# Dealing PEER's gathered rows out among the gate groups, and streaming the modulation matrix through MLPs and GLA

## The chip, the core and the metric

The kernel runs on one core of a Trainium2 chip. The time is the device microseconds of one execution; the profiled execution also has a span in its trace, from the first to the last instruction. TensorE is PE (its weight loads PEld), VectorE DVE, ScalarE ACT, GpSimd POOL, and SyncE, which issues most DMAs, SP.

## The reference

The program is two small networks in a row, batch 1, 256 positions, width 1024, all in fp32. The first has two layers (attention and MLP, then gated linear attention and MLP); the second two layers of a gated mixer and PEER, an expert layer that picks 16 of 16384 experts for each of 8 heads. Layer `l` of the second is modulated by a vector made from `c`:

```python
ada = (c @ w_ada[l] + b_ada[l])[:, None, :]
sh1, sc1, g1, sh2, sc2, g2 = jnp.split(ada, 6, axis=-1)
h = rmsnorm_2(x, norm1_g[l]) * (1.0 + sc1) + sh1
...                                             # mixer: x = x + g1 * (merged @ w_out[l])
h = rmsnorm_2(x, norm2_g[l]) * (1.0 + sc2) + sh2
x = x + g2 * peer(h, w_query[l], sub_keys[l], expert_u[l], expert_v[l])
# peer, per token t, over its picked experts (index idx, gate g):
u = jnp.take(expert_u, idx, axis=0); vv = jnp.take(expert_v, idx, axis=0)
a = jax.nn.gelu(jnp.einsum("td,thkd->thk", h, u))
out = jnp.einsum("thk,thkd->td", g * a, vv)
```

## The kernel before

**Weights.** Every weight comes in chunks of 128x1024 fp32 (`chunk`, L157 to L167): SP loads `raw` (4 buffers), ACT casts it to `whi` (L164), DVE subtracts to get `wlo` (L165; 3 buffers each), and PE runs three matmuls in place of one, hi by hi, hi by lo, lo by hi (L170 to L172). PE can't start a chunk's lo part before DVE has written `wlo`, and ACT can't cast chunk n before PE has left chunk n - 3.

**PEER.** Its experts are 128 blocks of 128. Positions 0 to 223 are computed densely: for each block, `u_block` makes all 128 dot products (24 matmuls of 224 columns) and ACT applies gelu into `A`; then the gates, zero for the experts that weren't picked, are multiplied into `A` (L1223); then `v_block` splits two blocks of `A` into hi (ACT, L223) and lo (DVE, L224), in `yh` and `yl`, and adds the products up in PSUM. The gates of 8 positions at a time are built by a group: three DVE operations (L1204, L1207, L1211), 16 small matmuls (L1221, L1222) and the multiplication; 28 groups for each half of the experts, listed in pairs. The last 32 positions go another way: 32 times, one row of `expert_u` is gathered for each of 128 (position, pick) pairs by an indirect DMA that POOL issues (L1113, tile `rows`, 3 buffers), and DVE makes a dot product of it with `hN` (L1124); `row_gates` applies gelu and the gates; 32 gathers of `expert_v` follow, which DVE adds up in `hN` (L1133, L1135); `rows_out` brings the sums into PSUM. The order is: 64 U blocks (U1), beside which DVE picks experts (top-16 steps, L941 to L945, and what follows); 64 U blocks (U2) beside the gates of the first half; 64 V blocks (V1) beside the gates of the second; 60 V blocks (V2); a tail of four whose chunks are loaded into buffers of their own.

**What sets the order around the change.** Side work waits in a list of steps, each with a cost (`Bg`). Each weight chunk adds a share (`U1_SHARE`, `MLP_SHARE`, ...) to a credit, and steps are taken off the front while the credit covers them; `flush` takes all that is left at once. A dot or a sum costs 1.05 and asks for the gather of two dots later when it is taken; the first three gathers are asked for together, and a step of 2.0 that does nothing follows them. A scheduler then places every engine's instructions with this program order as its priority. What is in the lists: in U1, the pick steps; in U2, the first half's gates, then 18 dots; in V1, the second half's gates; in V2, the 14 other dots, `row_gates` and 32 sums.

**The modulation vector.** `ada_steps` makes it from 96 chunks of `w_ada`, 48 a layer, in the same `raw` buffers: SP loads a chunk, and DVE multiplies it by `c` and adds up (L737) in one instruction; a second one reads the sum. A step costs 1.14. Layer 0's 48 steps run in both MLPs beside the weights' chunks; layer 1's are split, 36 from the second half of the last MLP through mixer 0, 12 at the end of the first PEER's V2. GLA (`gla`) sets the list aside for one of its own, which `flush` empties before its attention part; there, DVE's state updates (L674) and masked products (L682, L685) feed PE (L696).

Of the kernel before, what the change touches and what calls it, by code (L numbers as in the profile page):

```python
# [20 lines left out]
T = 256  # L21
# [19 lines left out]
MIX_SHARE = 0.45  # L41
U1_SHARE = 1.2
U2_SHARE = 1.25
V1_SHARE = 1.0
V2_SHARE = 0.9
DOTS1 = 18
ADA1 = 36
GSCALE = 2.0 ** 15
# [51 lines left out]
class Net:  # L100
# [378 lines left out]
    def mlp(self, l):  # L479
        nc, a = self.nc, self.a  # L480
        with ExitStack() as st:
# [23 lines left out]
            if l == 0:  # L505
                self.next_norm(self.gain(1))
            else:
                self.bg.flush()
                self.ada_steps(1, 0, ADA1, self.cb)
                self.next_norm(self.gg, self.modc(0, 0), self.tot2, self.gain(4))  # L510
# [3 lines left out]
    def gla(self):  # L514
        nc, a, c, tc = self.nc, self.a, self.cst, self.tc
        with ExitStack() as st:
# [119 lines left out]
            def ev_r(half):  # L636
# [9 lines left out]
                return go  # L646

            for half in range(2):
                ci = self.lin_nat(a["wgin"], ci, 512, self.yh, self.yl, ev_v(half), 1.2)
# [75 lines left out]
            self.next_norm(self.gain(3))  # L725
            self.lin(a["wgo"], 0, 8, 8, oh, ol, self.add_x, n=T)


    def ada_steps(self, l, i0, i1, cb):
        nc, a = self.nc, self.a  # L730
        cols = slice(l * 48, l * 48 + 48)

        def one(i):
            def go():
                raw = self.sp.tile([P, 1024], F32, tag="raw", name="raw", bufs=4)
                nc.sync.dma_start(out=raw, in_=a["wada"][i])
                nc.vector.tensor_tensor_reduce(out=raw, in0=raw, in1=cb, op0=ALU.mult, op1=ALU.add, scale=1.0,  # L737
                                               scalar=0.0, accum_out=self.mod[:, i : i + 1])
            return go

        def fin():
            nc.vector.tensor_add(out=self.mod[:, cols], in0=self.mod[:, cols], in1=self.cst["bada"][:, cols])
            for k, gi in ((1, 5), (4, 7)):
                m = self.modc(l, k)
                nc.vector.scalar_tensor_tensor(out=m, in0=m, scalar=1.0, in1=self.gain(gi + l),
                                               op0=ALU.add, op1=ALU.mult)
            if l == 0:
                nc.vector.tensor_mul(out=self.gg, in0=self.gain(4), in1=self.modc(0, 1))
        self.bg.add([(1.14, one(i)) for i in range(l * 48 + i0, l * 48 + i1)] + [(0.3, fin)] * (i1 == 48))

# [273 lines left out]
    def peer(self, l):  # L1024
        nc, a, c, tc = self.nc, self.a, self.cst, self.tc
        V = nc.vector
        with ExitStack() as st:
# [63 lines left out]
            def h_rows():  # L1091
# [7 lines left out]
                for k0 in (0, 4):  # L1099
# [5 lines left out]
                    nc.scalar.copy(out=hN[:, k0 * P : k0 * P + 512], in_=m)  # L1105

            def rows_of(name, use):

# [36 lines left out]
            with ExitStack() as s0:  # L1145
# [33 lines left out]
                self.wys.close()  # L1179
            self.bg.add(self.pick_steps(tm, fin))  # L1180

# [74 lines left out]
            self.set_banks(range(2, 8))  # L1256
            self.bg.add(gate_steps(0))
            dots = rows_of("un", dot)
            self.bg.add(dots[: DOTS1 + 2])
            for i2 in range(HALF, NI2):  # L1260
                u_block(i2, U2_SHARE)
            self.bg.flush()
            self.bg.add(gate_steps(1))
            vacc = [self.bank(2 + i).rearrange("p (k t) -> p k t", k=2) for i in range(4)]
# [8 lines left out]
            V.tensor_scalar_mul(g2s, self.modc(l, 5), 1.0 / GSCALE)  # L1273
            self.bg.add(dots[DOTS1 + 2 :] + [(0.5, row_gates)] + rows_of("ev", add_rows) + [(0.0, rows_out)])
            if l == 0:
                self.ada_steps(1, ADA1, 48, self.load(vp, "cb", eng=nc.sync))
            for i2 in range(HALF, NI2 - VTAIL):
# [36 lines left out]
    def run(self):  # L1314
# [10 lines left out]
        for name, f in stages:  # L1325
            f()
            if name == "att":
# [4 lines left out]
                cb = self.load(pool, "cb")  # L1332
                self.ada_steps(0, 0, 48, cb)
                self.cb = cb
            if name == self.stop:
# [139 lines left out]
```

## Time and profile before

| | us |
|---|---|
| median of three runs | 2587.16 |
| lowest and highest of them | 2585.8 and 2591.28 |
| the profiled execution | 2591.03 |
| its span in the trace | 2589.2 |
| PE busy in the span | 2526.5 |
| DVE busy in the span | 2112.0 |

PE is busy nearly all the time, so a view that averages over the span says little; the views to read are those of short stretches, where PE is idle or its granted clock is below 1.00. Matmuls overlap, so their single durations don't add up to time; how many of them run in a stretch does. In the trace the stages stand at: attention 0 to 95, MLP 95 to 295, GLA to 440, MLP to 640, mixer 0 to 800, PEER 0 to 1600 (U1 860 to 1034, U2 to 1222, V1 to 1415, V2 to 1585), mixer 1 to 1780, PEER 1 to the end.

### The profile page before, as it was taken

To read this page: it belongs to the slowest core of one execution; us is meant where nothing else is said; L and a number is where in the kernel's file an instruction comes from. 1 tells how busy PE (TensorE), PEld (TensorE's weight loads), DVE (VectorE), ACT (ScalarE), POOL (GpSimd) and SP (SyncE) were. 2 spreads that over 40 slices of the span, in tenths; PEclk is the share of its full clock that TensorE was granted. 3 is DMA by queue.
4 is the path that set the end of the run, shared out by engine and by line. 5 is a ranking of instruction groups with operands and counts; after the bars stand their busy time and mean duration, and the time that the engine had idled before them with its cause. 6 is when DMAs were issued, how large, how long until landed. Compare 5 with 4: busy or idle time off the path is not lost.

```text
span 2589.2 us, 55162 instructions
## 1 busy us (share of the span) xinstructions
PE 2526.5 (98%) x22496; PEld 2471.4 (95%) x22496; DVE 2112.0 (82%) x3835; ACT 1307.3 (50%) x2035; POOL 205.5 (8%) x172
## 2 busy tenths in 40 slices
PE   8999999999999999999999998999999999999998
PEld 7899988999999999999999997999999999999998
DVE  7787687877887798788887888778798788888886
ACT  6654475545546545444444544646545444444444
POOL 0000100000000000003000341000000002100341
PEclk9999999999999999999999998999999999999999
DMA  5288753876576566657656898465566667766895
GB/s 189 98 290 276 239 163 123 286 270 230 179 263 204 175 195 205 197 176 276 220 180 197 319 344 292 147 187 191 170 197 195 204 180 257 237 184 180 302 349 194
DMA packets 155918, 567.00 MB, mean 219 GB/s; under 512 B 17696, under 2 KB 17920, under 8 KB 155408
## 3 DMA queue, kind: packets, MB, share of 16 engines
q1 hardware_dynamic: 135792, 491.49, 58.7%
q0 software_dynamic: 19872, 71.99, 7.8%
q8 instruction: 176, 2.88, 0.5%
q14 instruction: 78, 0.64, 0.1%
HBM read 562.36 MB, written 1.05 MB: 218 GB/s over the span
## 4 chain that ended last, share of the span: by engine, by line
PE 74%; issue 15%; DMA 6%; DVE 3%; ACT 1%; POOL 1%; SPq 0%; DVEq 0%; POOLq 0%; ACTq 0%
PE b L170 23%; PE b L171 23%; PE b L172 23%; DMA rows<-in_ev,idx 3%; DVE wlo L165 1%; POOL rows L1113 1%; DMA raw<-in_wada 1%; DMA A<-in_sel 1%; ACT whi L164 1%; PE b L1169 1%; DMA rows<-in_un,idx 1%; DVE hN L1135 1%; PE b L1221 1%; PE b L1222 0%; PE b L825 0%
## 5 line engine op out<-in xcount | busy, mean ns | idle before, releaser
L170 PE MATMUL b<-yh,whi 128*128 128x224 f32 (+3 forms) x5336 | 1486.1, 279 | 12.6 <-ACT whi L164 9.0
L171 PE MATMUL b<-yl,whi 128*128 128x224 f32 (+3 forms) x5336 | 1480.1, 278 | 12.0 <-DVE yl L224 11.9
L172 PE MATMUL b<-yh,wlo 128*128 128x224 f32 (+3 forms) x5336 | 1481.1, 278 | 2.2 <-DVE wlo L165 2.2
L164 ACT CAST whi<-raw 128x1024 fp32r<-128x1024 f32 x829 | 867.9, 1049 | 1145.9 <-PE b L171 978.6
L165 DVE TENSOR_TENSOR wlo<-raw,whi 128x1024 fp32r<-128x1024 f32 x829 | 1010.8, 1221 | 245.3 <-ACT whi L164 237.9
L170 PEld LDWEIGHTS b<-yh,whi 128*128 128x128 f32 (+1 forms) x5336 | 1024.3, 192 | 16.8 <-ACT whi L164 9.5
L171 PEld LDWEIGHTS b<-yl,whi 128*128 128x128 f32 (+1 forms) x5336 | 1025.7, 192 | 15.3 <-DVE yl L224 12.6
L172 PEld LDWEIGHTS b<-yh,wlo 128*128 128x128 f32 (+1 forms) x5336 | 1024.3, 192 | 4.9 <-DVE wlo L165 3.4
L1113 POOL DMA_INDIRECT rows<-in_un,idx x64 | 82.9, 1295 | 1207.3 <-DVE wS L1124 759.5
L171 PE MATMUL b<-hl,whi 128*128 128x256 f32 x512 | 144.9, 283 | 0.0
L170 PE MATMUL b<-hh,whi 128*128 128x256 f32 x512 | 144.9, 283 | 0.0
L172 PE MATMUL b<-hh,wlo 128*128 128x256 f32 x512 | 144.9, 283 | 0.0
L737 DVE CUSTOM_DVE_ANT_0 raw<-raw,c_cb 128x1024 f32<-128x1024 f32 x96 | 117.1, 1220 | 7.5 <-DMA raw<-in_wada 7.3
L1113 POOL DMA_INDIRECT rows<-in_ev,idx x64 | 98.5, 1538 | 123.4 <-DVE hN L1135 92.4
L1223 DVE TENSOR_TENSOR A<-A,b 128x512 f32<-128x512 f32 x112 | 74.2, 684 | 36.9 <-PE b L1222 36.7
L171 PEld LDWEIGHTS b<-hl,whi 128*128 128x128 f32 x512 | 98.3, 192 | 0.0
L172 PEld LDWEIGHTS b<-hh,wlo 128*128 128x128 f32 x512 | 98.3, 192 | 0.0
L170 PEld LDWEIGHTS b<-hh,whi 128*128 128x128 f32 x512 | 98.3, 192 | 0.0
L1135 DVE SCALAR_TENSOR_TENSOR hN<-rows,wS,hN 128x1024 f32<-128x1024 f32 x62 | 79.4, 1281 | 18.8 <-DMA rows<-in_ev,idx 18.6
L1193 ACT ACTIVATE A<-b 128x224 f32<-128x224 f32 x256 | 89.6, 350 | 0.0
L1124 DVE CUSTOM_DVE_ANT_0 rows<-rows,hN 128x1024 f32<-128x1024 f32 x64 | 78.1, 1221 | 13.0 <-DMA rows<-in_un,idx 12.7
L1211 DVE TENSOR_TENSOR o<-oe,ghl 128x1024 f16<-128x1024 f16 x112 | 77.1, 689 | 1.7
(337 smaller groups left out, 2991.1 us busy)
## 6 DMA issues: line engine op xcount, KB each, us to landing
raw<-in_ut SPq DMA_DIRECT2D x256, 512.0 KB, 3.8
raw<-in_ev SPq DMA_DIRECT2D x256, 512.0 KB, 4.2
raw<-in_wada SPq DMA_DIRECT2D x96, 512.0 KB, 4.5
raw<-in_win SPq DMA_DIRECT2D x80, 512.0 KB, 4.0
raw<-in_wmi SPq DMA_DIRECT2D x64, 512.0 KB, 4.6
raw<-in_wmo SPq DMA_DIRECT2D x64, 512.0 KB, 4.6
raw<-in_wq SPq DMA_DIRECT2D x32, 512.0 KB, 3.6
raw<-in_wgin SPq DMA_DIRECT2D x24, 512.0 KB, 3.7
```

Source lines behind the costliest of these rows:

```text
L164: nc.scalar.copy(out=hi[:, :n], in_=raw[:, :n])
L165: self.last_lo = nc.vector.tensor_sub(out=lo[:, :n], in0=raw[:, :n], in1=hi[:, :n]).ins
L170: mm(out, lhsT=wh, rhs=yh, start=start, stop=False)
L171: mm(out, lhsT=wh, rhs=yl, start=False, stop=False)
L172: mm(out, lhsT=wl, rhs=yh, start=False, stop=stop)
L737: nc.vector.tensor_tensor_reduce(out=raw, in0=raw, in1=cb, op0=ALU.mult, op1=ALU.add, scale=1.0, scalar=0.0, accum_out=self.mod[:, i : i + 1])
L1113: nc.gpsimd.indirect_dma_start(out=got[g], out_offset=None, in_=a["un"] if name == "un" else a["ev"].rearrange("l i p d -> (l i p) d"), in ...
L1124: V.tensor_tensor_reduce(out=rows, in0=rows, in1=hN, op0=ALU.mult, op1=ALU.add, scale=1.0, scalar=0.0, accum_out=wS[:, g : g + 1])
L1135: V.scalar_tensor_tensor(out=hN, in0=rows, scalar=wS[:, g : g + 1], in1=hN, op0=ALU.mult, op1=ALU.add)
L1193: nc.scalar.activation(out=A[i2 // HALF][:, i2 % HALF, :], in_=ps[:, :NT], func=AF.Gelu_apprx_tanh)
L1211: V.tensor_tensor(out=o2, in0=e.unsqueeze(1).to_broadcast([P, 2, ng, HALF, GK]), in1=gates.to_broadcast([P, 2, ng, HALF, GK]), op=ALU.mult)
L1223: V.tensor_tensor(out=A[half][:, :, ts], in0=A[half][:, :, ts], in1=m.rearrange("p t i -> p i t"), op=ALU.mult)
```

## The change

Six things change.

- The steps of PEER's side work are listed otherwise. Six of the 32 dots follow the pick steps in U1; the other 26 are dealt out between the steps of the first half's gate groups in U2 (`mixed`); `row_gates`, the first three gathers and four sums are dealt out between the second half's gate groups in V1; V2 has the other 28 sums.
- The shares change with them: U1 1.2 to 1.35, U2 1.25 to 1.45, V1 1.0 to 1.12, V2 0.9 to 0.52.
- All 96 modulation steps are one list from the first MLP on, which runs on to the end of mixer 0; none is left in PEER.
- Eight of them move into GLA's own list, behind its 12 gate steps.
- GLA's output projection takes steps too (share 0.6).
- The last MLP's middle no longer empties the list, but takes steps only until layer 0's vector is done (`ada0`).

```diff
-U1_SHARE = 1.2
-U2_SHARE = 1.25
-V1_SHARE = 1.0
-V2_SHARE = 0.9
-DOTS1 = 18
-ADA1 = 36
+U1_SHARE = 1.35
+U2_SHARE = 1.45
+V1_SHARE = 1.12
+V2_SHARE = 0.52
+DOTS = (8, 24)
+SUMS = 4
+GLA_ADA = 8
...
-                self.bg.flush()
-                self.ada_steps(1, 0, ADA1, self.cb)
+                while not self.ada0:
+                    self.bg.q.pop(0)[1]()
...
+            self.bg.add(bg.q[:GLA_ADA])
+            del bg.q[:GLA_ADA]
...
-            self.lin(a["wgo"], 0, 8, 8, oh, ol, self.add_x, n=T)
+            self.lin(a["wgo"], 0, 8, 8, oh, ol, self.add_x, n=T, share=MLP_SHARE)
...
+            def mixed(steps, others):
+
+                n, out = len(others), []
+                for i, x in enumerate(steps):
+                    out.append(x)
+                    out += others[i * n // len(steps) : (i + 1) * n // len(steps)]
+                return out
...
-            self.bg.add(self.pick_steps(tm, fin))
+            dots = rows_of("un", dot)
+            self.bg.add(self.pick_steps(tm, fin) + dots[: DOTS[0]])
...
-            self.bg.add(gate_steps(0))
-            dots = rows_of("un", dot)
-            self.bg.add(dots[: DOTS1 + 2])
+            self.bg.add(mixed(gate_steps(0), dots[DOTS[0] :]))
...
-            self.bg.add(gate_steps(1))
+            sums = [(0.5, row_gates)] + rows_of("ev", add_rows)
+            self.bg.add(mixed(gate_steps(1), sums[: SUMS + 3]))
...
-            self.bg.add(dots[DOTS1 + 2 :] + [(0.5, row_gates)] + rows_of("ev", add_rows) + [(0.0, rows_out)])
-            if l == 0:
-                self.ada_steps(1, ADA1, 48, self.load(vp, "cb", eng=nc.sync))
+            self.bg.add(sums[SUMS + 3 :] + [(0.0, rows_out)])
...
-                self.ada_steps(0, 0, 48, cb)
-                self.cb = cb
+                self.ada0 = False
+                for l in range(2):
+                    self.ada_steps(l, 0, 48, cb)
```

DVE at the start of GLA's attention part, before, from the last weight chunks of wgin on; `rt` belongs to GLA's output gate, `st` is the state, `at` and `A` are the masked products that PE reads next:

```order
L165 TENSOR_TENSOR wlo<-raw,whi 128x1024 x3
L644 SCALAR_TENSOR_TENSOR sr<-rt,rt_4382 128x512
L674 SCALAR_TENSOR_TENSOR st<-st,eb,b_4410 128x256
L682 COPY_PREDICATED at<-c_gmask,b_4417 128x128
L644 SCALAR_TENSOR_TENSOR sr<-rt,rt_4387 128x512
L682 COPY_PREDICATED at<-c_gmask,b_4451 128x128
L165 TENSOR_TENSOR wlo<-raw,whi 128x1024
L674 SCALAR_TENSOR_TENSOR st<-st,eb,b_4403 128x256
```

The same place after; `L740` is a modulation step, in two instructions:

```order
L740 ISA raw,mod<-raw,c_cb 128x1024
L740 ISA mod 128x1
L677 SCALAR_TENSOR_TENSOR st<-st,eb,b_4427 128x256
L740 ISA raw,mod<-raw,c_cb 128x1024
L740 ISA mod 128x1
L677 SCALAR_TENSOR_TENSOR st<-st,eb,b_4434 128x256
L740 ISA raw,mod<-raw,c_cb 128x1024
L740 ISA mod 128x1
L645 SCALAR_TENSOR_TENSOR sr<-rt,rt_4388 128x512
L685 COPY_PREDICATED at<-c_gmask,b_4441 128x128
L685 COPY_PREDICATED at<-c_gmask,b_4475 128x128
```

Four more pairs of L740 rows stand directly ahead of these, behind the last wgin subtraction, so that seven steps stand among the first state updates; an eighth stands two weight chunks further on, just ahead of `A` (L688).

DVE at the end of U1, before, where the last pick steps write the indices of the rows to gather (`idx`) and the gates begin:

```order
L1076 TENSOR_TENSOR ghl<-A_9719,ghl 128x16x8
L165 TENSOR_TENSOR wlo<-raw,whi 128x1024 x2
L1204 TENSOR_TENSOR o_12879<-iotak,ix 128x1024
L1207 TENSOR_TENSOR oe<-iotak,ix 128x512
L1211 TENSOR_TENSOR o_12883<-oe,ghl 128x1024
```

And after, the same step (now L1080) and what follows it; `L1136` is a dot, in two instructions:

```order
L1080 TENSOR_TENSOR ghl<-A_9758,ghl 128x16x8
L166 TENSOR_TENSOR wlo<-raw,whi 128x1024
L1136 ISA rows,wS<-rows,hN 128x1024
L1136 ISA wS 128x1
L166 TENSOR_TENSOR wlo<-raw,whi 128x1024
L1136 ISA rows,wS<-rows,hN 128x1024
L1136 ISA wS 128x1
```

Six dots stand there, one ahead of each of the next chunks; the pick steps end six chunks sooner than before.

DVE in the middle of the V blocks, before: the last gate products (L1223), the dots (L1124), and the splits for the first blocks of V2 and of the tail (L224):

```order
L165 TENSOR_TENSOR wlo<-raw,whi 128x1024 x2
L1124 ISA rows,wS<-rows,hN 128x1024
L1124 ISA wS 128x1
L1223 TENSOR_TENSOR A_9719<-A_9719,b_18435 128x64x8
L1223 TENSOR_TENSOR A_9719<-A_9719,b_18453 128x64x8
L165 TENSOR_TENSOR wlo<-raw,whi 128x1024
L1124 ISA rows,wS<-rows,hN 128x1024
L1124 ISA wS 128x1
L224 TENSOR_TENSOR yl<-A_9719,yh 128x2x224 x4
L224 TENSOR_TENSOR twl<-A_9719,twh 128x224 x4
```

After, with the gate products as L1236, the sums as L1147 and the splits as L225:

```order
L166 TENSOR_TENSOR wlo<-raw,whi 128x1024 x2
L1147 SCALAR_TENSOR_TENSOR hN<-rows,wS,hN 128x1024
L1236 TENSOR_TENSOR A_9758<-A_9758,b_18465 128x64x8
L1236 TENSOR_TENSOR A_9758<-A_9758,b_18483 128x64x8
L166 TENSOR_TENSOR wlo<-raw,whi 128x1024
L225 TENSOR_TENSOR yl<-A_9758,yh 128x2x224 x3
L225 TENSOR_TENSOR twl<-A_9758,twh 128x224 x4
```

The last gate products stand two chunks sooner than before, counted in weight chunks, and the dot between them and the splits is gone.

## Rows read from the trace of the kernel before

**Rows 1.** The page: engines' busy time, and two of its groups of instructions.
```profile
PE 2526.5 (98%) x22496; PEld 2471.4 (95%) x22496; DVE 2112.0 (82%) x3835; ACT 1307.3 (50%) x2035; POOL 205.5 (8%) x172
...
L164 ACT CAST whi<-raw 128x1024 fp32r<-128x1024 f32 x829 | 867.9, 1049 | 1145.9 <-PE b L171 978.6
...
L737 DVE CUSTOM_DVE_ANT_0 raw<-raw,c_cb 128x1024 f32<-128x1024 f32 x96 | 117.1, 1220 | 7.5 <-DMA raw<-in_wada 7.3
```

**Rows 2.** Busy time by stretch: its length, each engine's busy us (instructions), PEclk, DMA.
```profile
760.00:785.00 25.00, 18.18 (x131) 17.68 (x130) 21.83 (x46) 9.69 (x15) 0.00 (x0) 0.86 0.83 281
866.00:938.00 72.00, 72.00 (x647) 72.00 (x647) 70.99 (x282) 36.13 (x56) 0.00 (x0) 1.00 0.65 201
1034.00:1190.00 156.00, 156.00 (x1715) 155.68 (x1714) 125.06 (x167) 69.09 (x106) 0.93 (x1) 1.00 0.60 188
1190.00:1232.00 42.00, 37.41 (x306) 36.86 (x306) 34.77 (x49) 18.85 (x29) 19.18 (x14) 0.92 0.92 330
1400.00:1424.00 24.00, 20.59 (x208) 20.25 (x205) 18.47 (x28) 9.67 (x15) 2.01 (x2) 0.93 0.64 201
...
1568.00:1602.00 34.00, 22.22 (x180) 21.86 (x180) 26.38 (x41) 8.83 (x10) 1.76 (x2) 0.80 0.90 308
2170.00:2212.00 42.00, 37.67 (x315) 37.49 (x315) 35.61 (x49) 18.95 (x31) 19.18 (x15) 0.92 0.93 336
2380.00:2404.00 24.00, 20.59 (x205) 20.25 (x202) 18.47 (x28) 9.70 (x15) 2.01 (x2) 0.93 0.66 198
2500.00:2560.00 60.00, 58.17 (x500) 57.51 (x499) 51.12 (x49) 27.00 (x31) 25.03 (x14) 0.97 0.93 334
```

**Rows 3.** Waits from 1195 to 1230: who waited for what, us in total, times, longest.
```profile
DVE rows L1124 <- DMA rows<-in_un,idx: 5.7, 5, 1.9
...
PE b L171 <- DVE yl L224: 3.9, 1, 3.9
```

**Rows 4.** DVE in order of time at U2's end: start, us, instruction, idle before.
```profile
1216.64 1.23 DVE L1124 CUSTOM_DVE_ANT_0 rows<-rows,hN 128x1024 f32<-128x1024 f32 x1 [1.91 <-DMA rows<-in_un,idx]
...
1217.80 1.22 DVE L165 TENSOR_TENSOR wlo<-raw,whi 128x1024 fp32r<-128x1024 f32 x1
...
1224.17 0.68 DVE L1204 TENSOR_TENSOR o<-iotak,ix 128x1024 f16<-128x1024 f16 x1
...
1225.11 1.69 DVE L224 TENSOR_TENSOR yl<-A,yh 128x448 fp32r<-128x448 f32 x3
```

**Rows 5.** DVE in order of time in the middle of the V blocks.
```profile
1414.85 1.28 DVE L1223 TENSOR_TENSOR A<-A,b 128x512 f32<-128x512 f32 x2
```

**Rows 6.** Waits from 1540 to 1605, the end of the first PEER.
```profile
ACT tvh L164 <- DMA raw<-in_ev: 17.4, 4, 15.5
```

**Rows 7.** SP's queue in order of time at mixer 0's end.
```profile
760.36 10.84 SPq L736 DMA_DIRECT2D raw<-in_wada  x7
```

**Rows 8.** Groups of DVE instructions from 866 to 938, part of U1.
```profile
L944 DVE MAX8 A<-A 128x8 f32<-128x128 f32 x32 | 9.2, 286 | 0.4
```

**Rows 9.** DVE in order of time at the start of GLA's attention part.
```profile
375.99 1.23 DVE L165 TENSOR_TENSOR wlo<-raw,whi 128x1024 fp32r<-128x1024 f32 x1 [1.57 <-ACT whi L164]
378.29 0.69 DVE L644 SCALAR_TENSOR_TENSOR sr<-rt,rt 128x512 f32<-128x512 f32 x1 [1.08 <-ACT rt L643]
...
383.49 0.49 DVE L685 TENSOR_TENSOR A<-at 128x128 f32<-128x128 f32 x2
```

**Rows 10.** POOL and DVE in order of time where the first rows are asked for.
```profile
1029.76 1.01 POOL L1113 DMA_INDIRECT rows<-in_un,idx  x1 [221.60 <-DVE ghl L1076]
...
1029.89 1.23 DVE L165 TENSOR_TENSOR wlo<-raw,whi 128x1024 fp32r<-128x1024 f32 x1 [0.56 <-ACT whi L164]
```

**Rows 11.** The gathered tile rows: first its issues from 1029 to 1042, then all.
```profile
DMA to landing us min/median/max: 5.3/7.3/8.4
...
DMA to landing us min/median/max: 4.2/6.8/9.6
```

**Rows 12.** PE in order of time at the start of GLA's attention part.
```profile
384.55 0.59 PE L696 MATMUL b<-v,A 128*128 128x256 f32 x2
```

More of the change, by code (lines that the diff above doesn't have):

```diff
@@ L748, in fin @@
                 nc.vector.tensor_mul(out=self.gg, in0=self.gain(4), in1=self.modc(0, 1))
+                self.ada0 = True
         self.bg.add([(1.14, one(i)) for i in range(l * 48 + i0, l * 48 + i1)] + [(0.3, fin)] * (i1 == 48))
```

## The prediction

> **What bounds the kernel now.** I read the page's busy line first, then the busy time of stretches, then the waits in those stretches where PE is not full, and last the DVE queue around them. PE is busy 2526.5 of 2589.2 us and DVE 82% of the span [rows 1], so the kernel is a PE stream and an edit can only win what PE does not use: 62.7 us of idle time, and the time lost when the granted clock is halved after an idle stretch. In the stretch 866 to 938, the first half of PEER's expert blocks (I call it U1), PE runs 647 matmuls in 72 us [rows 2], so a block of 24 takes 2.67 us; a stretch loses its idle time plus (1 - mean granted clock) times its length. Those losses sit in a few places [rows 2]. Mixer 0's end, 760 to 785: 25 - 18.2 = 6.8 idle, 0.14 x 25 = 3.5 by the clock. The end of the second half of U blocks (U2): 4.6 + 3.4 = 8.0, and 4.3 + 3.4 = 7.7 in the second layer. The middle of the V blocks: 3.4 + 1.7 = 5.1, and the same again in layer 1 at 2380 to 2404. The end of the first PEER: 11.8 + 6.8 = 18.6. The end of the second: 1.8 + 1.8 = 3.6.
>
> What ends these waits? At U2's end, PE waits 3.9 us for yl, which DVE writes [rows 3], and DVE is late because 18 dots were packed into one block each: five times in this stretch it waited for gathered rows, 5.7 us in all [rows 3], with the next weights' wlo behind the dot in its queue [rows 4]. In the middle of V, the last gate products (L1223) and a dot stand, from 1414.85 [rows 5], just ahead of the L224 splits that PE needs. At the end of the first PEER, ACT waits 15.5 us at once for V's last weights [rows 6], which stand behind ten modulation loads in SP's queue. At mixer 0's end seven such loads hold SP's queue for 10.8 us ahead of wout [rows 7].
>
> **The change part by part.** *The modulation matrix leaves PEER.* Twelve steps go from the first PEER's end to GLA and its output projection. Layer 1's PEER has no such steps and nothing like the 11.8 us gap; I count the 18.6 as won, less 1.0 for the hand-over to the tail: -17.6. What is late next is the gathered sum, dealt below. At mixer 0's end the order has six steps in the flush where it had seven, so that gap stays and shrinks by one step, about the 10.84 / 7 = 1.5 us of one load in SP's queue [rows 7]: -1.5.
>
> *Dots and sums dealt out.* U2 now has 26 dots, one per 2.5 blocks, each asked for two dots ahead, some 13 us, against the 9.6 us of the slowest landing [rows 11]. DVE is busy 125 of 156 us there while it does gates alone [rows 2]; 26 dots at 1.16 (from 1216.64 to the next row at 1217.80 [rows 4]) over a 185 us stage make it (148 + 30) / 185 = 96%, and a dot now falls where the gates leave a hole. No loss there, then. At the end of U2 the L224 still stands behind a wlo and two gate instructions (0.94 us, 1224.17 to 1225.11 [rows 4]), so about 1.0 us stays: -(8.0 + 7.7 - 2.0) = -13.7. If the cover fails, the old 8 stay. In V's middle the third place shown in the change's order has the last L1223 two blocks sooner and no dot between it and the splits, two blocks being 5.3 us against the 3.4 waited: -(2 x 5.1 - 0.2) = -10.0. In the last half of V a sum comes every second block (5.3 us) and no longer faster than its gather; I count the 3.6 of the second layer's end and 0.3 of the first: -3.9. Gains together: 17.6 + 1.5 + 13.7 + 10.0 + 3.9 = 46.7.
>
> *U1 at share 1.35 instead of 1.2.* DVE is busy 70.99 of 72 us there [rows 2]. Spread over the 27 blocks of that stretch, which hold 32 top-16 steps [rows 8], that is 2.63 us a block: 1.14 of wlo (1.22 long [rows 4], 0.08 of it under the next row, as 1216.64 + 1.23 is past 1217.80) and 1.49 for 1.2 steps. At 1.35 it is 1.14 + 1.68 = 2.82, or 2.86 if the gaps of 0.04 between rows stay, against 2.67. The top-16 part holds 47.6 of credit, 35 blocks, so DVE falls 5.3 to 6.7 us behind. It starts some 3.1 us ahead: ACT may cast two blocks early (5.34), less a cast of 1.05 [rows 1] and a subtraction of 1.2. PE pays the rest, 2.2 to 3.6, in pieces too short to cost the clock. I take 3.5 a layer, since the gaps do stay: +7.0. Bounds: 0, if the steps are shorter when they queue tightly, and 6.7.
>
> *The first dots.* Six dots now follow the indices at once (the second place shown), one a block. Their gathers start at 1029.76 of the old trace and after [rows 10], and land 5.3, 7.3 and 8.4 us later [rows 11], while the wlo that began at 1029.89 [rows 10], the one ahead of the first dot now, would end at 1031.1. The dot runs at 1035.1, the next wlo ends at 1037.5, about 0.6 after PE needs it; the second adds 0.5; from the third on a dot frees a buffer every block and the landing is covered. +1.1 a layer, +2.2; bounds 0 and 4 a layer (a first landing of 9.6).
>
> *GLA.* Of the eight steps given to GLA's own queue one finds credit; seven stand in a flush, and the first place shown has them on DVE ahead of the state updates (L674) and the products A (L685). A step takes 1.22 us [rows 1], 1.15 to the next row. From the last wgin subtraction (375.99) to A (383.49) [rows 9], DVE gets seven more steps there and one more further on, 9.2 us, and one more wlo, 1.1, less the 1.1 that it idles [rows 9]: 9.2. PE's matmuls that need no A run until 384.55 [rows 12], and in its order nothing else stands ahead of the one that does: 9.0 of idle time. Between the mixer's 6.8 idle (3.5 by the clock) and PEER's 11.8 (6.8) [rows 2], I take 4.0 for the clock: +13. Bounds: 3, if the steps find DVE idle (it has such holes later in the attention part), and 17, if their loads, four buffers deep, come late. The four steps in the output projection: 4 x 1.15 on a DVE with room: +1.0, 0 to 3.
>
> Costs: 7.0 + 2.2 + 13 + 1.0 = 23.2. The profiled execution took 2591.0 (2589.2 of span); 2591.0 - 46.7 + 23.2 = 2567.5. The median is 3.9 below that execution, so **2564 us**.
>
> **The rivals.**
> *The costs don't come* (0.18). U1's DVE work closes up when it queues, and GLA's steps fall into holes: costs of 5, so 2587.2 - 46.7 + 5 = 2546. For it: ACT leads by two blocks, and DVE is 82% busy in all. Against it: DVE at 98.6% in U1 [rows 2].
> *The ends stay* (0.10). The waits at U2's end and V's middle belong to the hand-over (yh and yl are shared, A must be complete), not to the queue. Then only 17.6 + 1.5 + 3.9 = 23.0 are won, against 23.2 paid: 2587, no change. For it: the L224 stands at the same place in U2's order as before. Against it: DVE's wait for rows is in the trace [rows 3, 4].
> *The change does not do what it says* (0.07). The steps aren't even: bursts stay in GLA, in mixer 0 and at U1's end. If each burst costs like the old ones (U1's end half of U2's 8.0, twice), 2564 + 6 = 2570.
> *Slower: gathers land late among the gates* (0.05). If each of 128 dots and sums in PEER waits in DVE's queue ahead of a wlo, PE pays. The five waits in U2's end average 1.1 us [rows 3]; 128 x 0.6 = 77 more would give 2564 + 77 = 2641; from 0.18 us each on it is slower than before. Place: DVE in U2 and V. For it: a landing took 4.2 us at best and 9.6 at worst [rows 11]. Against it: 9.6 is inside the lead of two dots. The Trainium skill ("SBUF — State Buffer", section "SBUF: two separate sides") says that a gather issued from GpSimd can be starved of descriptors while DVE runs in a two-port mode; the same page (section "Who interferes with whom") says that tensor_tensor, which the gate groups are made of, has no such mode. By the first this rival would decide, by the second it would not; no row here shows a gather held up by a gate.
>
> **How the numbers follow.** The forecast has 0.60, with its own range from 2554 (all gains, costs at 13) to 2578 (gains 8 less, costs 29). Faster by more than 0.2% (5.2 us, about what a measurement of this kernel can tell from no change) takes the forecast, the first and third rival and a third of the second: 0.88. Within 0.2%: 0.07. Slower: 0.05. The range from 2546 to 2580 holds the forecast, most of the first rival and the third; the second and the fourth, and the rest, some 2 in 10, are outside.
>
> **What would show it.** The gap of 11.8 us at the first PEER's end and DVE's waits for rows gone; in V's middle no wait of PE for yh or yl; one gap near 1 us at each U2 end. In GLA, PE waiting 7 to 10 us for A with L737's steps (L740 now) busy on DVE just before, and the clock halved after it. In U1 blocks 20 to 38, PE waiting for wlo in pieces of 0.1 to 0.6 us, with DVE full. At mixer 0's end a gap near 5 us. Wrong would be: no GLA gap (then 2551), U1's loss above 7 us a layer, or gathers that DVE waits for in U2.

## The result, and the profile after

The changed kernel takes 2557.87 us (median of 4 runs, 2554.61 to 2562.75) against 2586.63 before: a ratio of 0.9887, 95% interval 0.9864 to 0.9909, or 28.8 us less. The forecast was 2564, with 2546 to 2580 as its range. The profiled execution of after took 2562.75, its span 2560.4 us; before had 2591.03 and 2589.2, so the two traces differ by 28.3 and can be compared term by term.

PE's row on the page answers [rows 1]: idle time, 62.7 us before, is 43.8 now, and PE's busy time, which counts a slow matmul as longer, fell by 9.9 as well. Both come from fewer stalls, since the work is the same.

```profile
PE 2516.6 (98%) x22496; PEld 2461.7 (96%) x22496; DVE 2098.6 (82%) x3835; ACT 1301.5 (51%) x2031; POOL 182.3 (7%) x172
...
L740 DVE CUSTOM_DVE_ANT_0 raw<-raw,c_cb 128x1024 f32<-128x1024 f32 x96 | 116.9, 1219 | 3.5 <-DMA raw<-in_wada 3.4
```

Busy time by stretch answers [rows 2] (columns as there). In order: GLA's start, mixer 0's end, U1, the middle of U2, U2's end, V's middle, the first PEER's end, and V's middle in the second layer.

```profile
374.50:393.00 18.50, 15.32 (x65) 11.83 (x66) 16.82 (x35) 6.47 (x10) 0.00 (x0) 0.91 0.91 306
...
775.00:800.00 25.00, 19.14 (x144) 18.64 (x143) 19.25 (x46) 9.44 (x15) 0.00 (x0) 0.86 0.78 261
...
879.60:951.60 72.00, 72.00 (x647) 72.00 (x647) 71.79 (x309) 36.15 (x56) 0.00 (x0) 1.00 0.64 199
...
1050.00:1210.00 160.00, 160.00 (x1706) 159.72 (x1705) 145.86 (x202) 72.40 (x111) 29.25 (x23) 1.00 0.79 264
1215.00:1250.00 35.00, 33.99 (x366) 33.76 (x363) 29.35 (x43) 17.17 (x27) 3.93 (x4) 1.00 0.74 241
1410.00:1434.00 24.00, 24.00 (x240) 23.98 (x239) 20.64 (x26) 12.02 (x18) 3.09 (x3) 1.00 0.74 236
1570.00:1610.00 40.00, 40.00 (x350) 39.95 (x350) 29.85 (x51) 22.52 (x36) 0.00 (x0) 1.00 0.54 181
...
2370.00:2394.00 24.00, 24.00 (x237) 24.00 (x234) 19.80 (x25) 13.64 (x20) 4.15 (x4) 1.00 0.78 253
```

The reader should see three things. The stall at the first PEER's end (11.8 idle, clock at 0.80) and the one in V's middle are gone: PE fills those stretches at full clock. One microsecond is left at U2's end. GLA's start has lost 3.2 us of PE's time in 18.5, where before had no stall worth a row (PE busy 18.45 of the same 18.5), and mixer 0's end lost 5.9 where it had lost 6.8.

To put a size to each stage I compare when the same PE instruction (the n-th of 22,496) starts in both traces; the gates are dealt in another order, and so are the instructions at mixer 0's start, so only places outside both are used. A stage's size is how much the lag of after behind before changes over it.

| stage | forecast | measured |
|---|---|---|
| up to MLP0's end | 0 | +2.1 |
| GLA's attention part | +13 | +5.5 |
| output projection, MLP1's start | +1.0 | +3.6 |
| MLP1 | 0 | 0.0 |
| mixer 0's start | 0 | +2.1 |
| rest of mixer 0, its end | -1.5 | -1.4 |
| start of the first PEER | 0 | +1.6 |
| U1 and the first dots, both layers | +9.2 | +1.3 and +1.0 |
| U2's ends | -13.7 | -7.0 and -6.2 |
| V's middle | -10.0 | -5.5 and -5.5 |
| last half of V and first PEER's end | -17.9 | -15.8 |
| last half of V, second layer | -3.6 | -4.4 |
| mixer 1 | 0 | -0.2 |
| sum, before rounding | -23.5 | -28.7 |

This is one execution of each kernel. Four of the runs below (e2_ada, e4_u1_150, e6_u1_120, e8_u2_165) have the same PE instructions in the same order up to PEER, and so show how far a stage's size holds: in them GLA's attention part costs 5.3 to 7.9, the output projection 1.9 to 5.6, mixer 0's start 0.5 to 0.6 and PEER's start nothing.

### The profile page after: what moved, and what is told of

It is laid out like the page before. It is cut to its first block, busy times and chain, and to the rows that moved or that the text cites. A ratio compares the mean times of both kernels' runs of the same rounds, so it can differ in the third digit from the quotient of the medians.

```text
span 2560.4 us, 55126 instructions
## 1 busy us (share of the span) xinstructions
PE 2516.6 (98%) x22496; PEld 2461.7 (96%) x22496; DVE 2098.6 (82%) x3835; ACT 1301.5 (51%) x2031; POOL 182.3 (7%) x172
## 4 chain that ended last, share of the span: by engine, by line
PE 92%; DMA 3%; DVE 2%; ACT 1%; issue 1%; POOL 0%; SPq 0%; DVEq 0%; ACTq 0%
PE b L171 29%; PE b L173 29%; PE b L172 28%; PE b L1234 1%; PE b L1235 1%; DVE wlo L166 1%; DMA rows<-in_un,idx 1%; PE b L1181 1%; ACT whi L165 0%; DMA raw<-in_wmi 0%; PE b L829 0%; DMA raw<-in_wada 0%; DMA x<-in_xT 0%; PE b L426 0%; DMA A<-in_sel 0%
## 5 line engine op out<-in xcount | busy, mean ns | idle before, releaser
L171 PE MATMUL b<-yh,whi 128*128 128x224 f32 (+3 forms) x5336 | 1484.4, 279 | 12.1 <-ACT whi L165 11.4
L171 PEld LDWEIGHTS b<-yh,whi 128*128 128x128 f32 (+1 forms) x5336 | 1021.3, 192 | 17.5 <-ACT whi L165 12.7
L1125 POOL DMA_INDIRECT rows<-in_un,idx x64 | 88.7, 1387 | 698.7 <-DVE gS L1093 411.1
L740 DVE CUSTOM_DVE_ANT_0 raw<-raw,c_cb 128x1024 f32<-128x1024 f32 x96 | 116.9, 1219 | 3.5 <-DMA raw<-in_wada 3.4
L1125 POOL DMA_INDIRECT rows<-in_ev,idx x64 | 69.4, 1084 | 613.7 <-DVE hN L1147 374.4
L1236 DVE TENSOR_TENSOR A<-A,b 128x512 f32<-128x512 f32 x112 | 73.5, 682 | 21.5 <-PE b L1235 21.3
L1136 DVE CUSTOM_DVE_ANT_0 rows<-rows,hN 128x1024 f32<-128x1024 f32 x64 | 78.0, 1219 | 12.4 <-DMA rows<-in_un,idx 12.4
L1147 DVE SCALAR_TENSOR_TENSOR hN<-rows,wS,hN 128x1024 f32<-128x1024 f32 x62 | 79.3, 1279 | 0.0
```

The costliest lines, as they stand in the source:

```text
L171: mm(out, lhsT=wh, rhs=yh, start=start, stop=False)
L1125: nc.gpsimd.indirect_dma_start(out=got[g], out_offset=None, in_=a["un"] if name == "un" else a["ev"].rearrange("l i p d -> (l i p) d"), in ...
L1136: V.tensor_tensor_reduce(out=rows, in0=rows, in1=hN, op0=ALU.mult, op1=ALU.add, scale=1.0, scalar=0.0, accum_out=wS[:, g : g + 1])
L1147: V.scalar_tensor_tensor(out=hN, in0=rows, scalar=wS[:, g : g + 1], in1=hN, op0=ALU.mult, op1=ALU.add)
L1236: V.tensor_tensor(out=A[half][:, :, ts], in0=A[half][:, :, ts], in1=m.rearrange("p t i -> p i t"), op=ALU.mult)
```

## The experiments

Every kernel ran beside the kernel before on one chip; ratios are against it. The changed kernel was measured in one session alone, so a difference to its 2557.87 is good to some 3 us: the medians of before lie between 2586.63 and 2589.57 over the sessions.

**The two parts alone.** The first kernel keeps the dealing and puts the modulation back; the second does the reverse.

```diff
 e1_deal, against the changed kernel
-                while not self.ada0:
-                    self.bg.q.pop(0)[1]()
+                self.bg.flush()
+                self.ada_steps(1, 0, ADA1, self.cb)
...
+            if l == 0:
+                self.ada_steps(1, ADA1, 48, self.load(vp, "cb", eng=nc.sync))
```

> The changed kernel with its modulation part undone: dots and sums dealt among the gate groups, the four shares as changed, but the modulation steps where they were (36 of the second layer from MLP1 on, 12 in the first PEER's last V blocks and their flush). The prediction's terms for this part: U2 ends -13.7, V's middle -10.0, V's second half -3.9, U1 at 1.35 +7.0, first dots +2.2, sum -18.4, so about 2568. By the trace of the changed kernel (PE's position against the old trace, U1 and first dots +2.3, U2 ends -12.9, V's middle -10.7, second layer's last part -4.4, sum -25.7) it should be about 2561, with the gap of 11.8 us at the first PEER's end still there. A rival: that gap closes by the dealing of the sums too, at least in part; then under 2553.

```diff
 e2_ada, against the kernel before
-                self.bg.flush()
-                self.ada_steps(1, 0, ADA1, self.cb)
+                while not self.ada0:
+                    self.bg.q.pop(0)[1]()
...
+            self.bg.add(bg.q[:GLA_ADA])
+            del bg.q[:GLA_ADA]
...
-            if l == 0:
-                self.ada_steps(1, ADA1, 48, self.load(vp, "cb", eng=nc.sync))
```

> The kernel before with the modulation part alone: all 96 steps as one queue, eight of them in GLA, some in the output projection, none in PEER; dots, sums and shares as before. The prediction's terms: -17.6 -1.5 +13 +1.0 = -5.1, about 2582. By the trace of the changed kernel (before GLA +2, GLA +6, output projection +3.5, mixer 0's start +3, its end -1, PEER's start +1.5, first PEER's end -15.8) about 2586, no change that can be measured: what the first PEER wins is paid again in GLA and the mixer. The rival of the run beside it: if the sums, and not the modulation loads, kept V's last weights waiting, the gap at the first PEER's end stays here and the time is near 2602.

Measured: dealing alone 2564.2 us, ratio 0.9908 (0.9893 to 0.9923), 23.9 less than before; modulation alone 2581.2, ratio 0.9972 (0.9958 to 0.9985), 6.9 less. The first time lies between the two expected (2568 and 2561), the second at the prediction's terms (2582). The two gains add up to 30.8, against 28.8 for both together. Who closes the first PEER's end is plain from the two traces. Waits with the dealing alone, from 1555 to 1590, and the busy time of that stretch:

```profile
ACT tvh L165 <- DMA raw<-in_ev: 19.0, 4, 18.4
...
PE b L171 <- ACT tvh L165: 12.5, 1, 12.5
```
```profile
1555.00:1595.00 40.00, 27.50 (x219) 27.32 (x219) 28.46 (x42) 11.13 (x12) 2.13 (x3) 0.83 0.85 285
```

and busy time with the modulation alone: the same end, U2's end, V's middle.

```profile
1560.00:1600.00 40.00, 40.00 (x359) 39.90 (x358) 31.96 (x37) 21.08 (x28) 8.06 (x7) 1.00 0.83 295
1210.00:1236.00 26.00, 21.43 (x166) 20.86 (x165) 21.19 (x30) 10.66 (x18) 13.16 (x8) 0.89 0.87 319
1410.00:1430.00 20.00, 16.58 (x155) 16.25 (x154) 14.42 (x22) 8.35 (x14) 2.01 (x2) 0.91 0.62 204
```

With the dealing alone ACT still waits 18 us at once for V's last weights and PE 12.5; with the modulation alone PE is full there, although dots and sums are packed as before, and the waits of U2 and V are all still there. Each part closes its own stalls, as the prediction said.

**U1's share.** One line, 1.35 to 1.5:

```diff
-U1_SHARE = 1.35
+U1_SHARE = 1.5
```

> The changed kernel with U1's share at 1.5 instead of 1.35. It prices the DVE's work there, the term that the prediction had at +7.0 and the trace shows as nothing. As the prediction priced it (1.24 us a step and 0.04 of gaps): 1.14 + 1.86 + 0.04 = 3.04 us a block against 2.67, 0.37 over some 32 blocks is 11.7, less 3.1 of lead: 8.6 a layer, 2558 + 17 = 2575. As the trace of the changed kernel prices it (wlo's lead falls from 3.2 to 0.75 us in 35 blocks, 0.07 a block, so 1.185 a step): 2.92 a block, 0.25 over 32 blocks is 7.9 less 3.2: 4.7 a layer, 2567. If DVE's queue closes up without end: 2558, no change.

Measured: 2566.84, ratio 0.9923 (0.9909 to 0.9936). The number falls on the second reading, but the trace does not bear out its working: by PE's position U1 and the first dots together cost 1.9 in the first layer and 2.3 in the second, against 1.3 and 1.0 in the changed kernel: 1.9 more in all, not 4.7 a layer. The rest of the 9 us between the medians I can't place. The executions of the changed kernel run from 2554.61 (mean granted clock 0.997) to 2562.75 (0.995), and at the same 0.996 the two kernels stand at 2560.7 and about 2566. So a loss is likely, though the two intervals just meet; the price lies between 2 and 9, and the trace says 2.

What the trace does show is why both prices were too high. DVE in order of time, before (share 1.2), inside one block of U1:

```profile
888.18 0.28 DVE L941 MAX8 A<-A 128x8 f32<-128x128 f32 x1
888.49 0.09 DVE L942 MATCH_VALUE_LOAD A<-A 128x8 f32 x1
888.57 0.29 DVE L942 FIND_INDEX8 A<-A 128x8 uint32<-128x128 f32 x1
```

and with share 1.5 (the lines have moved by 4):

```profile
907.08 0.28 DVE L949 FIND_INDEX8 A<-A 128x8 uint32<-128x128 f32 x1
907.29 0.27 DVE L948 MAX8 A<-A 128x8 f32<-128x128 f32 x1
907.48 0.07 DVE L946 MATCH_VALUE_LOAD A<-A 128x8 f32 x1
```

In the first a search that needs the maximum just found starts 0.31 us after it, past its end. In the second two steps are mixed, so the next instruction needs nothing of the one ahead and starts 0.19 to 0.21 after it. The more steps stand in a block, the more such gaps close. The lead of wlo over the matmul that uses it tells what a step then costs: it stays near 3 us at share 1.2, falls from 3.19 (block 3) to 1.66 (block 26) at 1.35, and from 3.19 to 0.15 (block 24) at 1.5. With 2.67 us a block and 1.14 of wlo that makes 1.18 a step at 1.35 and 1.12 at 1.5, where the prediction carried 1.24 and 0.04 of gaps over from 1.2.

**U1 back at 1.2.**

```diff
-U1_SHARE = 1.35
+U1_SHARE = 1.2
```

> The changed kernel with U1's share back at 1.2, all 32 dots then in U2. If U1 at 1.35 costs what the prediction said (3.5 a layer), this wins 7: 2551. If, as the trace of the changed kernel and the run at 1.5 have it, wlo's lead just lasts at 1.35 (3.2 us fall to 0.75), nothing is won: 2558, and up to 4 more if U2's DVE now runs out of room for six more dots, which stand one a block in its last six blocks. The wait of DVE for the first gathered rows (3.8 us) should be there all the same, at U2's start.

Measured: 2578.94, ratio 0.9963 (0.995 to 0.9976): slower than the changed kernel by 21, which neither reading had. Waits from 1230 to 1245 and busy time of 1230 to 1262, at U2's end:

```profile
PE b L1234 <- DVE o L1224: 5.0, 3, 3.7
```
```profile
1230.00:1262.00 32.00, 26.49 (x253) 25.58 (x253) 25.84 (x38) 12.37 (x18) 0.76 (x1) 0.89 0.55 175
```

PE waits for the gates themselves (o), which now stand in the flush at U2's end, with the clock lowered behind the stall; PE's position says 11.0 us lost over U2 in the first layer and 12.7 in the second. What the run was made for it shows all the same: over U1, up to the first dots, PE's position against the changed kernel doesn't move, so U1's share of 1.35 costs nothing. Where the changed kernel has its first dots, this one wins 1.3 us in the first layer and 0.9 in the second, which is their price. DVE's wait for the first rows came as expected, now in U2, 3.9 us at the longest. For the loss at U2's end two readings are left: U2's share does not pay for six more dots, or DVE has no time for them. The next run raises the share of U2 alone:

```diff
-U1_SHARE = 1.35
-U2_SHARE = 1.45
+U1_SHARE = 1.2
+U2_SHARE = 1.65
```

> U1's share at 1.2 and all dots in U2, as in the run e6_u1_120 (2579), but U2's share at 1.65 instead of 1.45. Two readings of that run's loss of 21. Credit: U2 owes about 64 for its gates and 36 for 32 dots, 100 in all, and 64 blocks at 1.45 pay 93; the rest stands in the flush at U2's end, where PE waits for gates. At 1.65 it is paid by block 61 and nothing is left for the flush, not even the gap of 1.0 at U2's end: 2558 - 2 = 2556. Room: DVE has no time for 32 dots beside the gates (it was busy 151 of 168 us there), so a higher share only moves the wait to wlo inside U2, and the time stays above 2570.

Measured: 2559.27, ratio 0.9893 (0.9878 to 0.9908), as the changed kernel. It was the credit. DVE has time for the dots beside the gates, busy 154.92 of 160 us, and PE lost 0.2 there; at U2's end the wait for yl stayed, though. Busy time in U2, then DVE in order of time at its end:

```profile
1050.00:1210.00 160.00, 159.81 (x1716) 159.06 (x1715) 154.92 (x222) 70.51 (x108) 34.11 (x28) 1.00 0.83 277
```
```profile
1229.63 1.23 DVE L166 TENSOR_TENSOR wlo<-raw,whi 128x1024 fp32r<-128x1024 f32 x1 [1.45 <-ACT whi L165]
1230.78 0.68 DVE L1217 TENSOR_TENSOR o<-iotak,ix 128x1024 f16<-128x1024 f16 x1
1231.38 0.42 DVE L1220 TENSOR_TENSOR oe<-iotak,ix 128x512 f16<-128x512 f16 x1
1231.71 1.69 DVE L225 TENSOR_TENSOR yl<-A,yh 128x448 fp32r<-128x448 f32 x3
```

I had expected the gap of 1.0 to go. It stays because the two instructions ahead of L225 are the first gates of V, not a rest of U2: 0.93 us from 1230.78 to 1231.71.

**No bursts of modulation steps.** First the MLPs take them all, with a higher share:

```diff
-MLP_SHARE = 0.6
+MLP_SHARE = 0.8
-GLA_ADA = 8
+GLA_ADA = 0
...
-            self.lin(a["wgo"], 0, 8, 8, oh, ol, self.add_x, n=T, share=MLP_SHARE)
+            self.lin(a["wgo"], 0, 8, 8, oh, ol, self.add_x, n=T)
```

> The changed kernel with the modulation steps taken out of GLA (8 to 0) and out of the output projection (no share there), and the MLPs' share raised from 0.6 to 0.8, so that 43 steps go to each MLP, nine to mixer 0 and no flush is left at its end. The prediction's terms would give back 13 (GLA), 1.0 (output projection) and 8.8 (rest of mixer 0's end): 2558 - 23 = 2535. By the trace of the changed kernel GLA is worth 6, the output projection 3.5 and mixer 0's end 8.5: 2540. A rival: the MLPs cannot take the denser stream (DMA is at 0.77 there, and the loads share SP's queue with the weights), the waits come back as weights that land late, and the time stays near 2558.

Measured: 2557.9, ratio 0.9891 (0.9875 to 0.9906): nothing won, as the rival had it. Busy time in MLP0, in two halves, and the waits there:

```profile
110.00:215.00 105.00, 100.80 (x825) 98.94 (x824) 90.64 (x151) 54.71 (x101) 0.00 (x0) 1.00 0.82 274
215.00:318.00 103.00, 99.83 (x816) 97.96 (x816) 77.59 (x111) 42.93 (x55) 6.95 (x14) 1.00 0.88 292
```
```profile
ACT whi L165 <- DMA raw<-in_wmo: 46.3, 25, 3.8
ACT whi L165 <- DMA raw<-in_wmi: 37.5, 22, 3.2
```

In the changed kernel, over MLP0:

```profile
ACT whi L165 <- DMA raw<-in_wmi: 8.7, 8, 2.4
ACT whi L165 <- DMA raw<-in_wmo: 6.9, 4, 2.6
```

ACT waits 84 us for weights here, 16 in the changed kernel, and PE loses 11 us in MLP0 and 7 in MLP1 by its position, while GLA, the output projection and mixer 0 give back their share. The stall has moved from three bursts to many short waits. So the next kernel keeps the MLPs lower and takes what is left over to a place with room:

```diff
-MLP_SHARE = 0.6
+MLP_SHARE = 0.64
-V1_SHARE = 1.12
-V2_SHARE = 0.52
+V1_SHARE = 1.28
+V2_SHARE = 0.58
-SUMS = 4
-GLA_ADA = 8
+SUMS = 14
+GLA_ADA = 0
...
-            self.bg.flush()
-            if l == 0:
+            if l == 0:
+                self.rest, self.bg.q = self.bg.q, []
                 self.cbs.close()
+            self.bg.flush()
...
-            self.bg.add(sums[SUMS + 3 :] + [(0.0, rows_out)])
+            more = sums[SUMS + 3 :]
+            if l == 0:
+                self.cb = self.load(vp, "cb", eng=nc.sync)
+                more = mixed(more, self.rest)
+            self.bg.add(more + [(0.0, rows_out)])
```

The output projection has no share here either, the second layer's last V blocks have 0.36, and the steps read the table c_cb of the pool that is open.

> The changed kernel with no modulation step in GLA or the output projection and no flush at mixer 0's end: the MLPs at 0.64 (34 steps each, where 0.8 met the DMA's limit), what mixer 0 has no credit for (13 steps) spread singly over the first layer's last V blocks, and ten of the gathered sums moved from there to the V gates to make room. Two readings. If the price of the steps is that they stand in bursts (GLA 6 to 7.5, output projection 3.2, mixer 0 and PEER's start 10 or more in the trace of the changed kernel, against 0 to 2 for the MLPs): 2558 - 18 = about 2540; as the prediction priced them (13, 1.0 and 8.8): 2535. The rival: DMA is the limit wherever they are put (the last V blocks then carry weights, sums and steps, near 295 GB/s by my count), the waits come back there as V weights that land late, and the time is 2550 or more.

Measured: 2539.52, ratio 0.9817 (0.9799 to 0.9836): 18 below the changed kernel, at the first reading's 2540. PE's row, and busy time in the last half of V in the first layer:

```profile
PE 2509.2 (99%) x22496; PEld 2457.7 (97%) x22496; DVE 2097.3 (83%) x3835; ACT 1300.1 (51%) x2031; POOL 213.8 (8%) x172
```
```profile
1400.00:1560.00 160.00, 160.00 (x1436) 160.00 (x1435) 125.80 (x142) 77.26 (x90) 23.29 (x19) 1.00 0.85 292
```

There the DMA carries 292 GB/s, as in MLP0 above, and PE loses nothing. So the rate alone is not the limit. By PE's position all that this kernel wins lies ahead of PEER: 8.4 us in GLA and the output projection, 4.3 at mixer 0's start, 6.5 in the rest of mixer 0 and its end, 2.0 at PEER's start, less 0.8 lost before GLA. From there to the end the two kernels differ by 0.3, so the steps and sums that moved into V cost nothing there. Some 3.6 of the gain were not the steps' price: the changed kernel's trace is that much later at mixer 0's start and PEER's than the four runs with the same PE order. The steps left the bursts and the places at the same time; as many dealt singly inside GLA were not tried. Between MLP0 in the run at 0.8 and V here, what differs is that in MLP0 modulation loads and weights share SP's queue and its four raw buffers at 0.7 steps a block, and at 0.2 here; which of the two counts was not tried.

**GLA alone.** The same kernel with eight steps back in GLA:

```diff
-GLA_ADA = 0
+GLA_ADA = 8
```

> The kernel of the run e5_v2 with eight modulation steps put back into GLA, seven of them in the flush ahead of the attention part; everything else as there. The difference of the two is GLA's price alone. The prediction had 13 (9.0 idle, 4.0 by the clock); the trace of the changed kernel shows some 6 (3.2 idle around the state updates, 1.7 by the clock, the rest in short waits). If the steps found holes: 0 to 2.

Measured: 2543.46, ratio 0.9831 (0.9812 to 0.9849). The intervals of the two overlap, so 4 us is a likely price, not a proven one. By PE's position the steps cost 5.0 over the attention part, and 3.2 are left of it at PEER's start. The stretch 374 to 400, first without the steps:

```profile
374.00:400.00 26.00, 25.95 (x135) 19.61 (x135) 15.50 (x42) 11.70 (x26) 0.00 (x0) 1.00 0.35 100
```

then with them:

```profile
374.00:400.00 26.00, 22.77 (x107) 15.81 (x106) 20.54 (x45) 8.77 (x19) 0.00 (x0) 1.00 0.73 256
```

PE loses 3.2 us and the clock is not touched: 1.00 in both.

**Both together.** The kernel of e5_v2 with the shares of e8_u2_165:

```diff
-U1_SHARE = 1.35
-U2_SHARE = 1.45
+U1_SHARE = 1.2
+U2_SHARE = 1.65
```

> The kernel of the run e5_v2 (2539.5) with the two shares of the run beside it: U1 at 1.2, U2 at 1.65, all dots in U2. By the credit reading it wins the gap of 1.0 at each U2 end and the first dots' waits at U1's end (0.2 and 0.7 there in the trace of e5_v2): 2537 to 2539, hardly to be told from e5_v2. By the reading that DVE has no room: 2550 and more.

Measured: 2543.9, ratio 0.9831 (0.9815 to 0.9847), not to be told from e5_v2, and below the 2550 of the second reading. DVE has room, and nothing that these runs can tell was left to win in U1.

## Why the prediction was right, and where its sum was not

The sum, -23.5, is within 5.2 of the trace's -28.7, but two of its terms were far too dear and three stages were left out. The gains were right (45.8 measured, 46.7 forecast); the costs it named measured 11.4 where it had 23.2, and the stages it left out 5.6 where it had nothing. That these two partly cancel is luck.

- *The first PEER's end* (-17.6): right. The trace has -15.8 with the last half of V, and the two halves of the change run apart show that the modulation loads alone were the cause.
- *U2's ends* (-13.7) and *V's middle* (-10.0): right, -13.2 and -11.0. The wait for yl at U2's end is now 1.0 us, once in each layer, and for the reason given (two gate instructions of V ahead of L225). The rival in which the ends stay would have needed 8 there.

```profile
PE b L172 <- DVE yl L225: 1.0, 1, 1.0
```

- *V's last half* (-3.6 in the second layer): right, -4.4.
- *U1 at 1.35* (+7.0): the term that failed. The shortfall of DVE is there, wlo's lead falls block by block, but at 0.07 us a block and not 0.15 to 0.19, and the lead that remains is 0.7 us, so PE never waited in blocks 20 to 38, where the prediction looked for it. The step that was wrong is the price of a top-16 step, 1.24 us, read at a share at which the step's own gaps still stood open. The bound 0, for steps that queue tightly, was named and not taken.
- *The first dots* (+1.1 a layer): right, +1.3 and +1.0, which is all that the table's row has. DVE waits 3.8 us for the first rows, and of PE's loss in the first layer the view names 0.8 as a wait:

```profile
1032.43 1.23 DVE L1136 CUSTOM_DVE_ANT_0 rows<-rows,hN 128x1024 f32<-128x1024 f32 x1 [3.79 <-DMA rows<-in_un,idx]
```
```profile
PE b L173 <- DVE wlo L166: 0.8, 2, 0.6
```

- *GLA* (+13): the mechanism was right, the size not: +5.5, of it 3.2 idle and 1.7 by the clock. DVE in order of time, and PE beside it:

```profile
374.14 1.22 DVE L740 CUSTOM_DVE_ANT_0 raw<-raw,c_cb 128x1024 f32<-128x1024 f32 x1
...
381.38 0.48 DVE L677 SCALAR_TENSOR_TENSOR st<-st,eb,b 128x256 f32<-128x256 f32 x1
...
391.56 0.48 DVE L688 TENSOR_TENSOR A<-at 128x128 f32<-128x128 f32 x2
```
```profile
383.45 1.13 PE L670 MATMUL b<-vz,kn 128*128 128x256 f32 x4 [0.41 <-DVE st L677]
385.93 1.11 PE L684 MATMUL b<-qe,ke 128*128 128x128 f32 x4 [1.34 <-DVE at L685]
...
391.70 0.70 PE L670 MATMUL b<-vz,kn 128*128 128x256 f32 x2 [1.43 <-DVE st L677]
392.24 0.59 PE L699 MATMUL b<-v,A 128*128 128x256 f32 x2
```

A comes 8.1 us later on the clock than in [rows 9], 6 of it beyond the 2 that the kernel was late by then. The steps begin at 374.14, while PE still has the last wgin matmuls, so part of them is hidden; and PE's other matmuls (L670, L684) go on between the pieces. The step that failed is "nothing else stands ahead": of the 9.2 us of steps A came 6 later, and 3.2 became idle time. The sign named, PE waiting 7 to 10 us for A, did not come; PE waited for st and at, 3.1 us in all, and never for A. The clock term was taken from stalls whose longest pieces were 5.9 and 11.8 us, and here the longest piece is 1.4. Whether the clock falls there at all differs between traces of the same code, as the stretch 372 to 400 shows, first in the changed kernel, then in e8_u2_165:

```profile
372.00:400.00 28.00, 24.82 (x114) 18.58 (x113) 23.48 (x50) 10.12 (x21) 0.00 (x0) 0.94 0.80 267
```
```profile
372.00:400.00 28.00, 24.04 (x114) 17.28 (x113) 23.55 (x50) 10.48 (x21) 0.00 (x0) 1.00 0.78 271
```

- *The output projection* (+1.0): +3.6. I priced four DVE steps and forgot their loads, which stand in SP's queue ahead of the weights; PE waits for those weights. Waits from 375 to 465:

```profile
ACT whi L165 <- DMA raw<-in_wmi: 7.0, 6, 1.9
...
PE b L171 <- ACT whi L165: 4.3, 6, 1.0
ACT whi L165 <- DMA raw<-in_wgo: 4.1, 3, 2.6
```

- *Mixer 0's end* (-1.5): right, -1.4. The gap stayed, as forecast, 5.4 and 0.5 us, behind six loads in SP's queue:

```profile
772.08 11.21 SPq L739 DMA_DIRECT2D raw<-in_wada  x6
```

- *Left out*: MLP0's end, mixer 0's start (+2.1) and PEER's (+1.6). Most of it belongs to this execution and not to the change. At MLP0's end 1.5 of the +2.1 come where the clock is halved (see the last section), which the trace with the modulation part alone does not have. At mixer 0's start the clock is at 0.88 from 676 to 690; e6_u1_120 and e8_u2_165, with the same PE order, have 1.00 in the same place and lose 0.6. They too have the wait of 1.7 us for pT (L858) behind a chain of softmax steps on DVE, which came with the modulation part, so that wait cost little. At PEER's start DVE waited 1.9 us for the small table selo; the other runs of the same code do not show it.
- *The slower rival* (gathers land late among the gates) did not come. In U2 of the first layer, from 1046 to 1240, DVE waited once for rows, 0.8 us, and every landing took 5.2 to 6.4, less than the 6.8 of the median before. Over both layers DVE's waits for gathered rows are 12.4 us in nine waits, all at a layer's first dots, where before had 33.5 in thirty. In U2:

```profile
  DMA rows<-in_un,idx: 0.8, 1
...
DMA to landing us min/median/max: 5.2/5.6/6.4
```

The trace agrees with the second rule of the Trainium skill weighed there ("SBUF — State Buffer", section "Who interferes with whom"): gates made of tensor_tensor held up no gather. No run here shows whether the first, a gather starved beside a two-port mode, would hold.

## What to carry to other kernels

Price a queued step at the load at which it will run: a chain of short dependent instructions has gaps that close when a second chain is mixed in. Of a moved step count its loads before its arithmetic, and deal it singly; here the steps that stood in three bursts cost some 15 to 18 us more than the same steps dealt one by one to other places. Deal it thinly, too: in the MLPs alone, at 0.7 steps a block, the same steps won nothing. When a planner deals by credit, add up what a stage owes against its share before lowering any other stage's share.

## What the runs showed of the hardware

DVE: a small instruction that needs the result of the one ahead started 0.31 us after it (0.03 past its end), one that does not 0.20 after (0.08 before its end). A top-16 step has eight such instructions, three of which need the result of the one ahead. From share 1.2 to 1.5 it went from 1.24 to 1.12 us, about what one of the three gaps is worth.

The granted clock fell in MLP0's last microseconds to half for 3.4 us in some traces and not in others, with PE shown full. The stretches 318 to 322 and 322 to 330 in the changed kernel:

```profile
318.00:322.00 4.00, 4.00 (x17) 2.55 (x16) 0.00 (x0) 1.85 (x4) 0.00 (x0) 0.90 0.29 110
322.00:330.00 8.00, 8.00 (x59) 8.00 (x58) 3.72 (x5) 6.71 (x5) 0.00 (x0) 0.83 0.33 74
```

Before shows 1.00 in both. In this stage the run with the dealing alone has the code of before, and its trace has the drop; the run with the modulation alone has the code of the changed kernel, and its trace has none. GLA and mixer 0's start differ in the same way between traces of the same code (0.94 or 1.00, 0.88 or 1.00). Such drops are the likely reason why the executions of the changed kernel lie 8 us apart, with mean granted clocks from 0.995 (2562.75 us) to 0.997 (2554.61); what sets them off stays open.
